# Second parts of the unsummed weights from ACT's negated copy and an adding transfer, and another set of paired FFN tiles, in a two-layer hybrid decoder step

## The chip, the core and the metric

The kernel runs on one core of one Trainium2 chip. The metric is the device time of one execution in microseconds (us). The time before is 1921.07 us, the median of three runs (1919.98 to 1923.55).

The core's engines work side by side, each through its own queue in order, and wait for each other on semaphores: TensorE (PE in the profile, its weight loads PEld), VectorE (DVE), ScalarE (ACT), GpSimd (POOL) and SyncE (SP). Transfers between the device memory and the core's memory are issued from the queues of SP, POOL or ACT and run on DMA engines that all queues share.

## The reference

One step of two layers over 520 tokens (512 prompt, 8 sample) of 1024 features. Cut to what matters:

```python
def swiglu_ffn(x, wg, wu, wd):
    return (jax.nn.silu(x @ wg) * (x @ wu)) @ wd

def layer(x, ...):
    x = x + 0.5 * swiglu_ffn(rms_norm(x, p['ffn1_norm']), p['ffn1_wg'], p['ffn1_wu'], p['ffn1_wd'])
    z = rms_norm(x, p['mix_norm']) @ p['w_in']
    # retention, windowed attention and a convolution on pieces of z, joined, times w_out
    x = x + y
    return x + 0.5 * swiglu_ffn(rms_norm(x, p['ffn2_norm']), p['ffn2_wg'], p['ffn2_wu'], p['ffn2_wd'])
```

So there are four FFNs (two in each layer), with a hidden width of 2816, and a mixing stage in each layer. All is in float32.

## The kernel before

**Two parts.** Each float32 operand of a matmul is split into a first part, rounded to float32r, and a second part, which is the rest: source minus first part. A product is three matmuls: first by second, first by first, second by first. ACT makes the first part of a weight (`split_hi`, line 290), DVE the second (`split_lo`, line 296).

**Weights** arrive from device memory in chunks of 128 x 1024 by SP's queue (line 245), into four buffers, in the order in which they are used (`seq` lists the units). A buffer is loaded again when its last unit has been split (`done`). The parts lie in six slots of 128 x 1024 (tags `wh` and `wl`, three buffers each). A plain chunk takes two slots, one for each part. A unit of a paired product takes one: 512 columns of the first part, then 512 of the second. `ahead(u)` runs at the start of a unit: it queues the first parts of units up to six slots on, and the second parts of those that were pending before. So the splitting of a unit's weights can begin when the product six slots earlier has been done.

**An FFN** has 22 hidden tiles of 128 features and three down projections, over tiles 0 to 7, 8 to 15 and 16 to 21, that stand behind hidden tiles 8, 16 and 21. A plain hidden tile (`hidden`) is 16 weight blocks times six matmuls of 260 columns, 96 in all. A paired tile (`pair_hidden`, the tiles in `PAIRED`, and the first two down projections through `pair_down`, four times each) goes by a scheme with seven products in place of eight (`seven`): a11, s1, s2, a12, s3, s4, a22, each of 12 matmuls, 84 in all. Three of them (a11, a12, a22) use a block of the weights as it is; s1, s2 and s4 use sums of blocks that DVE makes (`sums`, lines 258 to 263), s2's subtraction in place in the raw chunk, which s3 then uses. The inputs need sums as well (`input_sums`, `pair_blocks`, `sums4`), which DVE makes, ACT splits and DVE splits again, in steps that `advance` puts between the products.

**Order around a paired tile.** `seven` copies the sums between products by ACT (lines 518, 525, 530); the next product but one adds to the copy, so TensorE waits for it. `late` (lines 554 to 557) runs on DVE after the sixth product: for each of the two results t and u an addition from PSUM and a multiplication by R. `last` (line 561) reads the other halves after the seventh. Then `gated` runs SiLU on ACT (line 428) and a multiplication on DVE (line 430). PSUM has four tiles, of which a paired tile uses three. In a plain tile DVE reads the two results at lines 443 and 444.

**POOL** issues the loads of constants (line 193, after the first FFN of a layer has done its paired tiles) and some loads and stores of the mixing stage. It has nothing in the other parts of the FFNs.

Of the kernel before, what the change touches and what calls it, by code (L numbers as in the profile page):

```python
# [10 lines left out]
F32 = mybir.dt.float32  # L11
F32R = mybir.dt.float32r
AF = mybir.ActivationFunctionType
ALU = mybir.AluOpType
# [6 lines left out]
FFN = 2816  # L21
NF = FFN // 128

PAIRED = (4, 5, 6, 8, 9, 10, 12, 13, 14, 16, 17, 18, 20, 21)


GROUPS = ((0, 8, True), (8, 16, True), (16, 22, False))
# [5 lines left out]
PC = JP * 128  # L33
# [76 lines left out]
def ffn_steps():  # L110


    steps = [("hidden", f) for f in range(NF)]
    for n, g in reversed(list(enumerate(GROUPS))):
        steps.insert(min(g[1] + 1, NF), ("down", n))
    return steps
# [20 lines left out]
def step_kernel(ctx: ExitStack, tc: tile.TileContext, io: dict):  # L137
    nc = tc.nc
# [56 lines left out]
    def wt(name, n=NT, dt=F32, bufs=None):  # L195
        return work.tile([128, n], dt, tag="t", name=name)
# [7 lines left out]
    seq, slot = [], [0]  # L204
# [7 lines left out]
    def add_products(n):  # L212
        for _ in range(n):
            for name in PRODUCTS:
                seq.append((name, chunk[0]))
                slot.append(slot[-1] + 1)
            chunk[0] += 2

    chunk = [0]
    for _ in range(DEPTH):  # L220
        for part in range(3):
# [3 lines left out]
            for step, n in ffn_steps():  # L225
                if step == "hidden" and n in PAIRED:
                    add_products(1)
# [7 lines left out]
    raw, done, spl, ready = {}, set(), {}, set()  # L235
    at, nxt, loaded, pending = [0, 0], [0], [0], []

    def load(dma=True):

        while loaded[0] < NCH and (loaded[0] < RAW or loaded[0] - RAW in done):  # L240
            i = loaded[0]
            loaded[0] += 1
            raw[i] = wraw.tile([128, CT * 128], F32, tag="w", name="w")
            if dma:
                nc.sync.dma_start(raw[i], io["w"][i])

    def sums(u):

        if u >= len(seq) or u in ready:
            return  # L250
        ready.add(u)
        name, i = seq[u]
        if name == "chunk":
            return
        load()
        (a21, a11), (a22, a12) = ((raw[j][:, :PC], raw[j][:, PC:]) for j in (i, i + 1))
        if name == "s1":
            nc.vector.tensor_add(Rd[:, 0, :PC], a21, a22)
        elif name == "s2":
            nc.vector.tensor_sub(a21, a21, a11)  # L260
            nc.vector.tensor_add(Rd[:, 1, :PC], a21, a22)  # L261
        elif name == "s4":
            nc.vector.tensor_sub(Rd[:, 0, :PC], a12, Rd[:, 1, :PC])  # L263

    def source(u):
        name, i = seq[u]
        if name == "chunk":
            return raw[i]
        if name[0] == "a":
            return dict(a11=raw[i][:, PC:], a12=raw[i + 1][:, PC:], a22=raw[i + 1][:, :PC])[name]  # L270
        return raw[i][:, :PC] if name == "s3" else Rd[:, int(name == "s2"), :PC]

    def parts_of(u):

        tag = ("wh", "wl")
        if seq[u][0] == "chunk":
            return tuple(wspl.tile([128, CT * 128], F32R, tag=t, name=t) for t in tag)
        t = tag[slot[u] % 2]
        w = wspl.tile([128, CT * 128], F32R, tag=t, name=t)
        return w[:, :PC], w[:, PC:]  # L280

    def split_hi():

        u = nxt[0]
        if u < len(seq):
            nxt[0] += 1
            load()
            sums(u)
            spl[u] = parts_of(u)
            nc.scalar.copy(spl[u][0], source(u))  # L290
            pending.append(u)

    def split_lo(n=9):
        for u in pending[:n]:
            h, lo = spl[u]
            nc.vector.tensor_sub(lo, source(u), h.bitcast(F32))  # L296
            name, i = seq[u]
            if name in ("chunk", "s3", "a22"):
                done.add(i + (name == "a22"))
                load()  # L300
        del pending[:n]

    def ahead(u):

        old = len(pending)
        while nxt[0] < len(seq) and slot[nxt[0] + 1] - slot[u] <= 6:
            split_hi()
        if seq[u][0] == "chunk":
            split_lo()
        else:  # L310
            split_lo(old)
            sums(nxt[0])
            sums(nxt[0] + 1)
# [108 lines left out]
    def flush():  # L422
        while advance():
            pass
# [8 lines left out]
    def hidden(norm, first):  # L433

        og, ou = ptile(), ptile()
        for i, (o, k) in enumerate(ffn_tiles(first, og, ou)):
            mm3(o, next_tile(), xh[:, k], xl[:, k], k == 0, k == KD - 1)
            if i % 2:
                advance()
        if first:  # L440
            run(norm)
        t, u = wt("t"), wt("u")
        nc.vector.tensor_mul(v2(t), og[:, :, :HN], v2(R))  # L443
        nc.vector.tensor_mul(v2(u), ou[:, :, :HN], v2(R))  # L444
        return t, u
# [67 lines left out]
    def seven(blocks, late, last, early=None):  # L513

        one, mid, c22 = ptile(), ptile(), ptile()[:, 0, :HN]
        c11, c21, m5, c12 = (t[:, i, :HN] for t in (one, mid) for i in range(2))
        product("a11", c11, blocks, True)
        nc.scalar.copy(c22, c11)  # L518
        advance()
        product("s1", m5, blocks, True)  # L520
        if early:
            early(m5)
        advance()
        product("s2", c22, blocks, False)
        nc.scalar.copy(c12, c22)
        advance()
        product("a12", c11, blocks, False)
        advance()
        product("s3", c22, blocks, False)
        nc.scalar.copy(c21, c22)  # L530
        advance()
        product("s4", c12, blocks, False)
        late(c12, c22, m5)
        advance()
        product("a22", c21, blocks, False)
        advance()
        last(one)
# [13 lines left out]
    def pair_hidden(blocks):  # L551
        t, u, v = wt("t"), wt("u"), wt("v")[:, :HN]

        def late(c12, c22, m5):
            for d, c in ((t, c12), (u, c22)):
                nc.vector.tensor_add(d[:, HN:], c, v)
                nc.vector.tensor_mul(d[:, HN:], d[:, HN:], R[:, HN:])

        def last(one):
            for i, d in enumerate((t, u)):  # L560
                nc.vector.tensor_mul(d[:, :HN], one[:, i, :HN], R[:, :HN])  # L561

        seven(blocks, late, last, lambda m5: nc.scalar.copy(v, m5))
        return t, u

    def ffn(l, name, norm, after):
        hs, even, spare, xs = {n: [] for n in range(len(GROUPS))}, None, [], []
        for step, n in ffn_steps():
            if step == "hidden":
                g = next(i for i, (a, b, _) in enumerate(GROUPS) if a <= n < b)  # L570
                t, u = pair_hidden(xs) if n in PAIRED else hidden(norm, n == 0)
                flush()
# [29 lines left out]
    def mix(l, after):  # L602
# [586 lines left out]
        def chunk_hi():  # L1189
            while True:  # L1190
                split_hi()
                yield

        def chunk_lo():
            while True:
                split_lo(1)
                yield
# [70 lines left out]
    for step in START:  # L1268
        if step[0] == "h":
            half(half_split, int(step[1]))  # L1270
        elif step[0] == "c":
            split_hi()
            split_lo()
        elif step[0] == "x":
            next(parts[int(step[1])])
            next(parts[int(step[1])])
        else:
            run(parts[int(step[1])])
# [17 lines left out]
def host_arrays(i):  # L1296
# [17 lines left out]
    for t, j in zip(gu, (1, 2)):  # L1314
# [3 lines left out]
        for step, n in ffn_steps():  # L1318
            if step == "hidden":
                g = t[:, n]  # L1320
                if n in PAIRED:

# [96 lines left out]
```

## Time and profile before

| | |
|---|---|
| median of three runs | 1921.07 us |
| the profiled execution | 1921.25 us |
| its span, first to last instruction | 1919.5 us |
| mean granted TensorE clock | 0.986 |
| read from device memory, written | 179.50 MB, 7.45 MB |

The span is what the trace covers; 1.75 us of the profiled execution lie around it. A row of a group gives line, engine, operation, result and operands, shapes and count, then the busy time in us and the mean of one in ns, then the idle time of the engine just before these instructions and what ended most of it. A row of the waits gives the engine and line that waited, what it waited for, the total in us, how often, and the longest. A row of the timeline gives start and duration in us, and in brackets the idle time before. A row of the chain gives start and length in us, engine, line and count. Matmuls overlap in the records: the duration of one is longer than the distance to the next.

### The profile page before, as it was taken

The numbers are of one execution on the slowest core, as the hardware profiler recorded it, in microseconds if no ns is written. First come the engines' busy times: TensorE is split into PE (matmuls) and PEld (weight loads), VectorE is DVE, ScalarE is ACT, GpSimd is POOL, SyncE is SP. The second block draws the span as 40 slices with busy tenths as digits, with TensorE's granted clock in tenths as the row PEclk, the third lists the DMA queues.
The fourth block names the chain that finished last, engine by engine and source line by source line (L and its number), as shares of the span: only waits on it lengthen the run. The fifth ranks groups of instructions, "written<-read, shape, count | busy, mean of one in ns | idle before, by whom it ended". The sixth has DMA issues, their size and how long they took to land.

```text
span 1919.5 us, 37036 instructions
## 1 busy us (share of the span) xinstructions
PE 1844.9 (96%) x15134; PEld 1820.6 (95%) x15134; DVE 1584.9 (83%) x2743; ACT 999.2 (52%) x1880; POOL 23.3 (1%) x52
## 2 busy tenths in 40 slices
PE   8999999999989999999999999999998999999999
PEld 8999999999989999999999999999998999999998
DVE  8988998688667998998779989976886579888984
ACT  6544545433765555555455555555238555455552
POOL 0000000000100000000000000000000000000000
PEclk9999999999999999999999999999999999999999
DMA  5233333433313133333323232334333132232332
GB/s 180 78 90 99 100 99 111 138 108 114 116 38 96 56 101 109 97 91 100 110 78 89 89 110 89 120 112 127 100 116 100 45 99 73 83 111 89 102 97 89
DMA packets 54171, 189.36 MB, mean 99 GB/s; under 512 B 6272, under 2 KB 7152, under 8 KB 54000
## 3 DMA queue, kind: packets, MB, share of 16 engines
q1 hardware_dynamic: 50784, 177.35, 30.4%
q0 software_dynamic: 3072, 9.53, 1.5%
q8 instruction: 119, 1.95, 0.4%
q14 instruction: 52, 0.43, 0.1%
q10 hardware_dynamic: 144, 0.11, 0.0%
HBM read 179.50 MB, written 7.45 MB: 97 GB/s over the span
## 4 chain that ended last, share of the span: by engine, by line
PE 76%; DVE 16%; ACT 5%; issue 2%; DMA 1%; ACTq 0%; POOL 0%; DVEq 0%; POOLq 0%
PE o L342 40%; PE o L334 34%; DVE wl L296 2%; DVE m L474 2%; DVE wh L296 2%; DVE Rd L263 1%; DVE u L430 1%; DVE w L260 1%; ACT wh L290 1%; DVE m L502 1%; ACT wl L290 1%; ACT t L428 1%; PE o L361 1%; DVE u L444 1%; DVE Rd L261 0%
## 5 line engine op out<-in xcount | busy, mean ns | idle before, releaser
L334 PE MATMUL o<-m,wl 128*128 128x260 f32 x2688 | 370.4, 288 | 24.0 <-DVE t L443 10.6
L334 PE MATMUL o<-m,wh 128*128 128x260 f32 x2688 | 366.3, 286 | 24.1 <-ACT o L518 19.0
L334 PEld LDWEIGHTS o<-m,wl 128*128 128x128 f32 x2688 | 346.0, 193 | 29.7 <-issue 11.4
L342 PE MATMUL o<-xl,wh 128*128 128x260 f32 x1792 | 364.4, 285 | 6.7 <-DVE xl L387 5.9
L290 ACT CAST wh<-w 128x512 fp32r<-128x512 f32 (+1 forms) x318 | 257.1, 810 | 217.0 <-PE o L342 154.8
L334 PEld LDWEIGHTS o<-m,wh 128*128 128x128 f32 x2688 | 343.2, 191 | 27.4 <-ACT o L518 20.9
L342 PE MATMUL o<-xh,wl 128*128 128x260 f32 x1792 | 362.0, 284 | 0.1
L342 PE MATMUL o<-xh,wh 128*128 128x260 f32 x1792 | 361.8, 283 | 0.0
L342 PEld LDWEIGHTS o<-xl,wh 128*128 128x128 f32 x1792 | 277.9, 189 | 8.1 <-ACT wh L355 5.9
L342 PEld LDWEIGHTS o<-xh,wl 128*128 128x128 f32 x1792 | 277.5, 189 | 0.4 <-DVE wl L296 0.4
L342 PEld LDWEIGHTS o<-xh,wh 128*128 128x128 f32 x1792 | 277.0, 189 | 0.0
L296 DVE TENSOR_TENSOR wl<-w,wh 128x1024 fp32r<-128x1024 f32 x142 | 173.3, 1221 | 34.2 <-ACT wh L290 31.9
L342 PE MATMUL o<-m,wh 128*128 128x260 f32 x1024 | 164.5, 282 | 4.1 <-DVE m L510 4.1
L342 PEld LDWEIGHTS o<-m,wh 128*128 128x128 f32 x1024 | 140.0, 188 | 4.9 <-DVE m L510 4.9
L290 ACT CAST wl<-w 128x512 fp32r<-128x512 f32 x176 | 108.7, 618 | 54.3 <-PE o L342 34.0
L428 ACT ACTIVATE t<-t 128x520 f32<-128x520 f32 x88 | 56.1, 637 | 137.1 <-DVE t L561 136.9
L334 PE MATMUL o<-xh,wl 128*128 128x260 f32 x672 | 124.6, 283 | 0.0
L334 PE MATMUL o<-xh,wh 128*128 128x260 f32 x672 | 124.3, 282 | 0.0
L296 DVE TENSOR_TENSOR wh<-w,wh 128x512 fp32r<-128x512 f32 x176 | 120.1, 682 | 0.0
L296 DVE TENSOR_TENSOR wl<-w,wl 128x512 fp32r<-128x512 f32 x176 | 120.1, 682 | 0.0
L290 ACT CAST wh<-Rd 128x512 fp32r<-128x512 f32 x132 | 82.0, 621 | 68.4 <-PE o L334 29.8
L290 ACT CAST wl<-Rd 128x512 fp32r<-128x512 f32 x132 | 81.8, 620 | 64.6 <-PE o L334 37.7
(216 smaller groups left out, 2716.5 us busy)
## 6 DMA issues: line engine op xcount, KB each, us to landing
w<-in_w SPq DMA_DIRECT2D x318, 512.0 KB, 3.6
out_y<-x SPq DMA_DIRECT2D x8, 260.0 KB, 2.0
m<-in_cm POOLq DMA_DIRECT2D x4, 512.0 KB, 4.3
m<-in_s_ret SPq DMA_DIRECT2D x4, 512.0 KB, 5.1
m<-sc POOLq DMA_DIRECT2D x8, 256.0 KB, 4.4
out_o_rets<-m POOLq DMA_DIRECT2D x4, 512.0 KB, 3.5
x<-in_x SPq DMA_DIRECT2D x3, 520.0 KB, 6.9
w<-in_w SPq DMA_DIRECT2D x4, 256.0 KB, 5.2
```

Source lines behind the costliest of these rows:

```text
L260: nc.vector.tensor_sub(a21, a21, a11)
L263: nc.vector.tensor_sub(Rd[:, 0, :PC], a12, Rd[:, 1, :PC])
L290: nc.scalar.copy(spl[u][0], source(u))
L296: nc.vector.tensor_sub(lo, source(u), h.bitcast(F32))
L334: nc.tensor.matmul(o, lhsT=a[:, s], rhs=b, start=first and j == 0 and i == 0, stop=j == JP - 1 and i == 2, skip_group_check=True,)
L342: nc.tensor.matmul(o[:, s, :HN], lhsT=a, rhs=b[:, s * HN : (s + 1) * HN], start=first and i == 0, stop=last and i == 2,)
L361: nc.tensor.matmul(o[:, s, :HN], lhsT=w, rhs=v[:, s * HN : (s + 1) * HN], start=i == 0, stop=i == len(parts) - 1,)
L428: nc.scalar.activation(t, t, AF.Silu)
L430: nc.vector.tensor_mul(u, u, t)
L444: nc.vector.tensor_mul(v2(u), ou[:, :, :HN], v2(R))
L474: nc.vector.tensor_sub(tl[:, c], src, th[:, c].bitcast(F32))
L502: nc.vector.tensor_sub(lo, a, h.bitcast(F32))
```

## The change

For a11, a12 and a22, `split_hi` now has ACT write a second copy, of the source times -1, into the place of the second part. Rounded to float32r it is the negated first part. Then a transfer issued from POOL adds the same block of the weights from device memory onto it (`accum_op`), which leaves the weights minus the first part. `split_lo` no longer subtracts on DVE for these units. The sources of s1, s2, s3, s4 and of plain chunks are split as before.

`PAIRED` has 15 tiles in place of 14, and others: 5, 6, 7, 9 to 15 and 17 to 21. Plain are now 0 to 4, 8 and 16 (before: 0 to 3, 7, 11, 15 and 19). The host lays the weights out for it.

In `late`, both additions run before the two multiplications.

```diff
-PAIRED = (4, 5, 6, 8, 9, 10, 12, 13, 14, 16, 17, 18, 20, 21)
+PAIRED = (5, 6, 7, 9, 10, 11, 12, 13, 14, 15, 17, 18, 19, 20, 21)
...
             nc.scalar.copy(spl[u][0], source(u))
+            name, i = seq[u]
+            if name[0] == "a":
+                nc.scalar.activation(spl[u][1], source(u), AF.Copy, scale=-1.0)
+                i, c = i + (name != "a11"), 0 if name == "a22" else PC
+                nc.gpsimd.dma_start(spl[u][1], io["w"][i][:, c : c + PC], accum_op=ALU.add)
             pending.append(u)
...
             h, lo = spl[u]
-            nc.vector.tensor_sub(lo, source(u), h.bitcast(F32))
             name, i = seq[u]
+            if name[0] != "a":
+                nc.vector.tensor_sub(lo, source(u), h.bitcast(F32))
...
             for d, c in ((t, c12), (u, c22)):
                 nc.vector.tensor_add(d[:, HN:], c, v)
+            for d in (t, u):
                 nc.vector.tensor_mul(d[:, HN:], d[:, HN:], R[:, HN:])
```

## The prediction

> **What bounds the kernel now.** I read the page's busy times first, then its groups, then TensorE's own waits, then windows stage by stage, and last the timeline at one stall. From the page:
>
> ```profile
> PE 1844.9 (96%) x15134; PEld 1820.6 (95%) x15134; DVE 1584.9 (83%) x2743; ACT 999.2 (52%) x1880; POOL 23.3 (1%) x52
> ...
> L334 PE MATMUL o<-m,wl 128*128 128x260 f32 x2688 | 370.4, 288 | 24.0 <-DVE t L443 10.6
> L334 PE MATMUL o<-m,wh 128*128 128x260 f32 x2688 | 366.3, 286 | 24.1 <-ACT o L518 19.0
> ...
> L290 ACT CAST wl<-w 128x512 fp32r<-128x512 f32 x176 | 108.7, 618 | 54.3 <-PE o L342 34.0
> L428 ACT ACTIVATE t<-t 128x520 f32<-128x520 f32 x88 | 56.1, 637 | 137.1 <-DVE t L561 136.9
> ...
> L296 DVE TENSOR_TENSOR wh<-w,wh 128x512 fp32r<-128x512 f32 x176 | 120.1, 682 | 0.0
> L296 DVE TENSOR_TENSOR wl<-w,wl 128x512 fp32r<-128x512 f32 x176 | 120.1, 682 | 0.0
> ```
>
> TensorE is busy 96% of the span, so nothing can win more than its idle time, its half-clock stretches, and matmuls left out. The idle time that this change can touch stands before the paired products of L334: 24.0 + 24.1 = 48.1 us. TensorE's waits name who ends it:
>
> ```profile
> PE o L334 <- ACT o L518: 19.0, 8, 2.4
> PE o L334 <- DVE u L556: 13.2, 15, 1.0
> PE o L334 <- DVE t L443: 10.6, 4, 2.9
> ...
> PE o L334 <- ACT o L530: 3.2, 8, 0.4
> PE o L334 <- ACT o L525: 2.1, 7, 0.3
> ```
>
> Those are 42 stops. ACT is named most, though it is busy 52%; the timeline where the first down projection begins shows what holds it (DVE rows, then ACT, then PE):
>
> ```profile
> 112.73 0.69 DVE L296 TENSOR_TENSOR wl<-Rd,wl 128x512 fp32r<-128x512 f32 x1
> 113.34 0.69 DVE L296 TENSOR_TENSOR wh<-Rd,wh 128x512 fp32r<-128x512 f32 x1
> ...
> 115.00 0.43 DVE L557 TENSOR_TENSOR t<-t,R 128x260 f32<-128x260 f32 x1
> 115.34 0.42 DVE L556 TENSOR_TENSOR u<-o,v 128x260 f32<-128x260 f32 x1
> ...
> 116.14 1.30 DVE L474 TENSOR_TENSOR m<-u,m 128x520 fp32r<-128x520 f32 x2
> 117.37 0.69 DVE L296 TENSOR_TENSOR wl<-w,wl 128x512 fp32r<-128x512 f32 x1
> 117.97 0.42 DVE L561 TENSOR_TENSOR t<-o,R 128x260 f32<-128x260 f32 x1
> ```
>
> ```profile
> 118.42 0.64 ACT L428 ACTIVATE t<-t 128x520 f32<-128x520 f32 x1 [3.84 <-DVE t L561]
> ...
> 119.47 0.37 ACT L518 COPY o<-o 128x260 f32<-128x260 f32 x1
> ```
>
> ```profile
> 115.82 1.71 PE L334 MATMUL o<-m,wl 128*128 128x260 f32 x12 [1.02 <-DVE u L556]
> 119.89 0.80 PE L334 MATMUL o<-m,wh 128*128 128x260 f32 x2 [2.36 <-ACT o L518]
> ```
>
> DVE runs without a break and late: a weight subtraction (117.37) stands ahead of L561, SiLU on ACT waits 3.84 us for L561, the copy L518 is queued behind SiLU, and TensorE waits 2.36 us for the copy. So the bound behind these stops is DVE's backlog in paired stretches. The windows say so by stage (columns: length, busy us of PE, PEld, DVE, ACT, POOL, then granted clock, DMA share, GB/s):
>
> ```profile
> 158.88:244.84 85.96, 84.24 (x698) 83.62 (x697) 77.36 (x144) 46.05 (x95) 0.00 (x0) 1.00 0.34 99
> 113.20:158.90 45.70, 42.32 (x339) 41.90 (x338) 40.87 (x72) 22.45 (x44) 0.00 (x0) 0.96 0.31 93
> 830.70:874.90 44.20, 40.81 (x339) 40.39 (x338) 40.70 (x72) 22.45 (x44) 0.00 (x0) 1.00 0.33 96
> 54.80:70.60 15.80, 12.90 (x87) 12.72 (x86) 14.71 (x27) 10.29 (x22) 0.00 (x0) 0.78 0.21 67
> ```
>
> DVE is busy 77.36 of 85.96 us over FFN tiles 9 to 16 (six paired), 14.71 of 15.80 over the first paired tile. A stop also costs granted clock: two equal down projections took 45.70 us at clock 0.96 and 44.20 at 1.00.
>
> **The change, part by part.**
>
> ```profile
> 179.19 11.53 PE o L342 x96
> 837.41 57.75 PE o L334 x480
> ```
>
> *One more paired tile in each of four FFNs.* A plain tile is 96 matmuls, 11.53 us; a paired one 84, at 57.75/480 = 0.120 us each 10.1 us. 4 x 1.45 = **5.8 us less** TensorE work.
>
> *DVE's subtraction goes for a11, a12, a22.* Each set of seven products loses three of 682 ns; queued ones start 0.60 us apart (112.73, 113.34), so 1.8 us a set. For tiles 9 to 16, then seven paired: TensorE needs 7 x 10.1 + 11.5 = 82 us; DVE 77.4 - 6 x 1.8 + about 3.6 (a plain tile made paired: four small subtractions, five sums and six short evictions for two long subtractions and two evictions) = 70 us, 86% where it had 90%, and the down projection falls from 40.9 by 4 x 1.8 to 33.7 us of 40.3. Backlogs drain within a tile instead of over four. The first paired tile is now the sixth: its 10.6 us of waits on L443 meet a DVE that had one more plain tile to catch up.
>
> *What the stops are worth.* 48.1 us are counted from the modelled end of the matmul before; a matmul lasts 0.286 and the next could start after 0.120, so each of the 42 stops hides 0.166 more: 7 us. Half clock: 1.5 us (45.70 against 44.20) in about five of eight down projections, and 0.22 of 15.80 us in the first paired tile, partly under idle time, four times: estimate 12 us together. At stake: 48 + 7 + 12 = 67 us. I let 10 stay (alternate tiles still carry four or more microseconds of input sums on DVE).
>
> A rule of the Trainium skill speaks against the 12: "TensorE: Matmul & The Clock Gate", section "HAM oscillation", says that only idle gaps over about 3.4 us bring the clock down. The longest stop above is 2.9 us and the clock is down at 0.96 and 0.78 around such stops, so the trace disagrees; by the Trainium skill's rule the 12 us would stay, and the sum be 1876.
>
> *`late` reordered.* The second L556 starts one L557 sooner: 0.34 us (115.00 to 115.34) at up to 15 stops, part of the 13.2 us above, not counted again.
>
> *ACT's negated copy.* 92 sets x 3 = 276 more instructions. None has this form in the trace; nearest are the cast of equal size, 618 ns, and an ACTIVATE, 637. I take 0.62; queued casts start 0.52 apart (108.92, 109.44 below). That is 1.6 us a set. Tiles 9 to 16: 46.0 + 21 x 0.52 + about 3 for the new paired tile = 60 of 82 us, so there is room. But ACT is in order: the copies L518, L525, L530 and SiLU come up to 0.5 us later. TensorE has one product (12 x 0.12 = 1.44 us) between a copy's input and its use, which covers it; without cover, 0.5 us x 92 sets = 46 us. I take 3.
>
> *The accumulating transfer.* It waits for the negated copy and TensorE's third matmul of the product waits for it. POOL has nothing else in the FFNs but the two constant loads after the first FFN's paired tiles; what queues behind a waiting issue is the next accumulate. SP's loads share the 16 DMA engines: share 0.34 at 99 GB/s, to which 3 x 262 KB per 10.1 us (78 GB/s) add 0.27 if plain, 0.54 if reading the destination counts double. So there is room, with queueing. What matters is the time from ACT to use:
>
> ```profile
> 106.09 0.60 ACT L290 CAST wl<-w 128x512 fp32r<-128x512 f32 x1
> ...
> 106.87 0.62 ACT L290 CAST wh<-w 128x512 fp32r<-128x512 f32 x1
> ...
> 108.92 0.62 ACT L290 CAST wl<-Rd 128x512 fp32r<-128x512 f32 x1
> 109.44 0.62 ACT L290 CAST wh<-Rd 128x512 fp32r<-128x512 f32 x1
> ```
>
> ```profile
> 111.77 1.61 PE L334 MATMUL o<-m,wl 128*128 128x260 f32 x12
> 113.21 0.28 PE L334 MATMUL o<-m,wh 128*128 128x260 f32 x1
> ```
>
> The cast of a22 ends at 106.69; a22's product starts at 111.77, its third matmul 0.24 later: 5.3 us. Less 0.52 for the negated copy: 4.8, and some 0.1 for waking: **4.7 us** from POOL's issue to the landing. The next a11 (106.87 to 113.45) has 5.96, less two copies, 4.9. In a down projection SiLU and the copy of v aren't ahead: about 1 us more, 5.8.
>
> ```profile
> m<-sc POOLq DMA_DIRECT2D x8, 256.0 KB, 4.4
> out_o_rets<-m POOLq DMA_DIRECT2D x4, 512.0 KB, 3.5
> ```
>
> ```profile
> DMA to landing us min/median/max: 3.4/4.4/5.8
> ```
>
> ```profile
> DMA to landing us min/median/max: 2.9/3.5/4.2
> ```
>
> No accumulate is in the trace. These are the page's rows of POOL's transfers, then the same two lines' own views (L1015, L1027): 256 KB in bursts of four land in 3.4 to 5.8 us, 512 KB alone in 2.9 to 4.2. An accumulate of 256 KB reads 512 KB: I take 4.0 us, nearest the lone 512 KB, and add 3 us over the kernel for late ones. Ends: 2.9 costs nothing, and none can gain, since only a late one is seen; 5.8 costs (5.8 - 4.7) x 60 hidden sets = 66 us, all of the gain; beyond the rows it can be more.
>
> The Trainium skill, "DMA: Bandwidth & Descriptors", section "Anatomy of one DMA", gives 2.0 us plus bytes over 436 GB/s: an estimate of 2.6 us for 256 KB, 3.2 for 512. The lone 512 KB rows lie at and above it; by it no transfer would be late and the sum would be 3 us lower. No run here shows an accumulate.
>
> **The sum.** The profiled execution took 1921.25 us: 1919.5 span and 1.75 around it, 0.2 over the median of 1921.07. 1921.3 - 5.8 - 67 + 10 + 3 + 3 = **1864.5 us**.
>
> **The rivals.**
> (a) *Slower: the accumulates land late.* Slot u's second part can't be begun until the product six back is done, so lateness isn't absorbed by a deeper queue: TensorE stops once a set. For it: 4.7 us is close to the 4.4 median, two issues 0.8 us apart overlap, SP's 512 KB share the engines, and an adding transfer may run below a copy's rate. Against: lone transfers land well inside. It decides from a landing of 4.7 + 57/60 = 5.65 us. At 7.0 (twice 3.5): 2.3 x 60 + 1.2 x 32 = 176 us, 1864.5 + 176 = 2040.
> (b) *Somewhat late*, landing at 5.2: 0.5 x 60 = 30, 1895.
> (c) *ACT takes the place of DVE.* The 24.3 us of stops that ACT ends (19.0 + 3.2 + 2.1) stay, with some 10 of the 7 + 12 us that go with stops: 1864.5 + 35 = 1900. For it: ten weight casts a set in one ordered queue with SiLU. Against: 60 of 82 us, and its 3.84 us wait was for DVE.
> (d) *Given back*: landing near 5.6, or long waits that move: 1921.
> (e) *The clock doesn't recover*: the half-clock stretches have another cause than these stops and stay, 1864.5 + 12 = 1876. That one of two equal stages was spared (44.20 against 45.70 us) with the same stops speaks for it, that they begin around stops against it. The rule of the Trainium skill above is this rival's.
> (f) *The backlog wasn't it*: stops come from a fixed chain of latencies. DVE's unbroken rows from 112.73 on speak against it; only 5.8 + 5 go: 1910. Counted with (c).
>
> **Chances.** Forecast 0.45 (1844 to 1885: 1848.5 with every stop gone and nothing late, 5 below for gaps too short for the rows; 20 above for twice the stops left and 10 us of lateness); (a) 0.21; (b) 0.14; (c) and (f) 0.09; (d) 0.07; (e) 0.04. Two kernels closer than 0.2% (3.8 us) can't be told apart. Faster 0.45 + 0.14 + 0.09 + 0.04 = 0.72, same 0.07, slower 0.21. The range 1844 to 1937 takes in all but most of (a).
>
> **What would show it.** Right: no L296 row for w of 512 columns but s3's 92; L334's idle time near 10 us and no L518 wait over 1 us; DVE near 1440 us busy, ACT near 1150; 276 new POOL issues landing near 4 us; clock 1.00 in the down projections. Wrong: TensorE's waits released by those transfers; many stops of equal length, one a set, at a22's or a11's third matmul (a); L518 still ahead in its waits while SiLU no longer waits for DVE (c). I would be wrong above all if an adding transfer takes over 5.6 us.

## The result, and the profile after

| | time, us | ratio to before |
|---|---|---|
| before, median of 4 | 1920.76 | 1 |
| changed, median of 4 | 1983.84 (1978.28 to 1986.45) | 1.0322, 95% interval 1.0308 to 1.0336 |

The changed kernel is 3.2% slower; 1864.5 us was forecast, and the time lies outside the range. The page of the changed kernel (its line 342 is the old 334, 350 the old 342, 305 the old 296; 295 is the negated copy, 297 the adding transfer):

```profile
span 1984.6 us, 37952 instructions
...
PE 1853.9 (93%) x15086; PEld 1815.2 (91%) x15086; DVE 1450.6 (73%) x2519; ACT 1156.3 (58%) x2192; POOL 262.0 (13%) x328
...
q1 hardware_dynamic: 50784, 177.35, 30.7%
q0 software_dynamic: 42816, 81.90, 24.6%
...
w<-in_w SPq DMA_DIRECT2D x318, 512.0 KB, 3.7
wh<-in_w POOLq DMA_DIRECT2D x138, 256.0 KB, 5.9
wl<-in_w POOLq DMA_DIRECT2D x138, 256.0 KB, 6.0
```

DVE and ACT are as busy as the prediction said (about 1440 and 1150 us). But TensorE, which has 48 matmuls fewer, idles 131 us of the span where it idled 75, and the adding transfers land in 5.9 to 6.0 us, not 4.0. TensorE's waits in the changed kernel:

```profile
PE o L342 <- DMA wl<-in_w: 55.5, 47, 2.3
PE o L342 <- DMA wh<-in_w: 48.8, 45, 2.0
...
PE o L342 <- ACT o L526: 3.5, 12, 0.4
```

The old waits for DVE's `t` and `u` before paired products are gone, and of those for ACT's copies 3.5 us are left. In their place stand 92 waits for the transfers, 104.3 us. Taken transfer by transfer, 85 of them (101.5 us) are at a22's product, each in another of the 92 sets of seven products; five are at a11's and two at a12's. With the 0.166 us that each stop hides (as worked out in the prediction) that is 104.3 + 92 x 0.166 = 119.6 us. The time measured is 1983.8 - 1864.5 = 119.3 us over the forecast. So the loss by the transfers is of the size of the whole miss; that the two agree this closely is partly luck, as e2 below shows.

One set in the timeline of the changed kernel, hidden tile 10: first ACT, then POOL, then SP, then TensorE.

```profile
175.78 0.61 ACT L290 CAST wh<-w 128x512 fp32r<-128x512 f32 x1
176.29 0.63 ACT L295 ACTIVATE wh<-w 128x512 fp32r<-128x512 f32 x1
```

```profile
177.22 0.86 POOL L297 DMA_DIRECT2D wh<-in_w  x1 [5.72 <-ACT v L572]
178.54 0.86 POOL L297 DMA_DIRECT2D wl<-in_w  x1 [0.45 <-ACT o L533]
183.92 0.86 POOL L297 DMA_DIRECT2D wh<-in_w  x1 [4.52 <-ACT wh L295]
```

```profile
174.93 2.35 SPq L245 DMA_DIRECT2D w<-in_w  x2
```

```profile
183.32 0.39 PE L342 MATMUL o<-m,wh 128*128 128x260 f32 x1 [0.95 <-DMA wh<-in_w]
```

a22's copy is done at 176.92, POOL issues at 177.22, 0.30 us later where 0.1 was allowed. TensorE stops until 183.3, at the third matmul of a22. SP's two weight loads of 512 KB go out between 174.93 and 177.28. The landing of the three transfers above, in order, each from the view of its own line and moment:

```profile
DMA to landing us min/median/max: 6.1/6.1/6.1
DMA to landing us min/median/max: 6.1/6.1/6.1
DMA to landing us min/median/max: 4.0/4.0/4.0
```

a22's and the next a11's take 6.1, a12's 4.0. The first two lie beside SP's loads, the third alone. It is so throughout: in all 92 sets two loads were in flight when a22's transfer was issued, the later one sent 0.27 us (median) before it. By the trace's issues and landings the medians are 6.3 us for a22's transfers, 6.4 for a11's and 4.25 for a12's.

### The profile page after: what moved, and what is told of

Its sections match the earlier page's. It is cut to its first block, busy times and chain, and to the rows that moved or that the text cites. A ratio compares the mean times of both kernels' runs of the same rounds, so it can differ in the third digit from the quotient of the medians.

```text
span 1984.6 us, 37952 instructions
## 1 busy us (share of the span) xinstructions
PE 1853.9 (93%) x15086; PEld 1815.2 (91%) x15086; DVE 1450.6 (73%) x2519; ACT 1156.3 (58%) x2192; POOL 262.0 (13%) x328
## 3 DMA queue, kind: packets, MB, share of 16 engines
q1 hardware_dynamic: 50784, 177.35, 30.7%
q0 software_dynamic: 42816, 81.90, 24.6%
## 5 line engine op out<-in xcount | busy, mean ns | idle before, releaser
L342 PE MATMUL o<-m,wl 128*128 128x260 f32 x2784 | 388.5, 286 | 56.2 <-DMA wl<-in_w 54.4
L342 PE MATMUL o<-m,wh 128*128 128x260 f32 x2784 | 388.1, 286 | 50.0 <-DMA wh<-in_w 47.8
L350 PE MATMUL o<-xl,wh 128*128 128x260 f32 x1664 | 337.9, 284 | 6.8 <-DVE xl L395 5.8
L350 PEld LDWEIGHTS o<-xl,wh 128*128 128x128 f32 x1664 | 257.4, 189 | 8.0 <-ACT wh L363 5.8
L350 PEld LDWEIGHTS o<-xh,wl 128*128 128x128 f32 x1664 | 257.0, 189 | 0.3 <-DVE wl L305 0.3
L350 PEld LDWEIGHTS o<-xh,wh 128*128 128x128 f32 x1664 | 256.8, 189 | 0.0
L297 POOL DMA_DIRECT2D wl<-in_w x138 | 119.7, 867 | 708.9 <-ACT wl L295 486.5
L297 POOL DMA_DIRECT2D wh<-in_w x138 | 119.7, 868 | 624.4 <-ACT wh L295 308.2
L350 PE MATMUL o<-m,wh 128*128 128x260 f32 x1024 | 164.1, 282 | 0.0
L550 DVE SCALAR_TENSOR_TENSOR x<-o,x 128x520 f32<-128x520 f32 (+1 forms) x128 | 72.0, 563 | 71.8 <-PE o L342 70.7
L305 DVE TENSOR_TENSOR wh<-Rd,wh 128x512 fp32r<-128x512 f32 x138 | 94.9, 688 | 37.2 <-ACT wh L290 35.6
```

The source lines that it names most:

```text
L297: nc.gpsimd.dma_start(spl[u][1], io["w"][i][:, c : c + PC], accum_op=ALU.add)
L342: nc.tensor.matmul(o, lhsT=a[:, s], rhs=b, start=first and j == 0 and i == 0, stop=j == JP - 1 and i == 2, skip_group_check=True,)
L350: nc.tensor.matmul(o[:, s, :HN], lhsT=a, rhs=b[:, s * HN : (s + 1) * HN], start=first and i == 0, stop=last and i == 2,)
L550: nc.vector.scalar_tensor_tensor(d, src, 0.5, d, op0=ALU.mult, op1=ALU.add)
```

## The experiments

All from the changed kernel, unless said. The theory at first was that the loss is lateness, from sharing the DMA engines; the rivals were the set of tiles, the adding itself, and POOL's issue path.

**e1, no adding transfers.** The new set and the new order in `late`, with all second parts by DVE.

```diff
-            if name[0] == "a":
+            if name in ():
...
-            if name[0] != "a":
+            if name not in ():
```

> The new set of paired tiles and the new order in late, all second parts by DVE again, no adding transfers. Theory T (the loss is lateness of the adding transfers, which share the DMA engines with SP's weight loads; the set itself is harmless): no stop by a transfer; DVE needs some 11.5 us a paired tile against 10.1 on TensorE, so seven in a row run late, but the first paired tile's 16 us are gone: 1905 to 1930 us. Rival S (the set with seven paired tiles in a row is what costs): 1950 us or more.

1896.9 us, ratio 0.9869 (0.9855 to 0.9884): faster than before by 1.3%, and 8 us better than the best end expected. The set is no cost. The granted clock is 0.995 here, where it was 0.986 before. DVE's backlog still stops TensorE, less than before:

```profile
PE o L342 <- DVE u L564: 12.5, 16, 1.3
PE o L342 <- DVE t L451: 10.0, 8, 1.5
PE o L342 <- ACT o L526: 10.0, 9, 1.2
```

So rival S falls. From before to e1, TensorE's busy time falls by 15.4 us, of which the forecast gave 5.8 to the matmuls left out, and its idle time from 74.6 to 65.0 us. From the page of e1:

```profile
PE 1829.5 (97%) x15086; PEld 1802.5 (95%) x15086; DVE 1594.2 (84%) x2795; ACT 1017.4 (54%) x1916; POOL 23.3 (1%) x52
```

**e2, a11 and a12 by transfers, a22 by DVE.**

```diff
-            if name[0] == "a":
+            if name in ("a11", "a12"):
...
-            if name[0] != "a":
+            if name not in ("a11", "a12"):
```

> As the changed kernel, but a22's second part by DVE again; 184 adding transfers instead of 276. T: the stop at a22's third matmul (about 1.1 us, 92 times) is gone, a11's transfer no longer has a neighbour 1.3 us away and lands in about 5 us instead of 6.4: 1870 to 1905 us. Rival A (an adding transfer is slow by itself, whatever lies beside it): a11 lands at 6.4 us and takes over a22's stops: 1950 us or more.

1868.33 us (1867.23 to 1869.45), ratio 0.9718 (0.9702 to 0.9734): better than both kernels, and 1.7 us under the range expected. The page's landings are

```profile
wh<-in_w POOLq DMA_DIRECT2D x92, 256.0 KB, 4.2
wl<-in_w POOLq DMA_DIRECT2D x92, 256.0 KB, 4.4
```

and TensorE's waits at the paired products are

```profile
PE o L342 <- DMA wh<-in_w: 5.6, 11, 1.3
PE o L342 <- DMA wl<-in_w: 5.3, 8, 1.1
PE o L342 <- ACT o L526: 4.7, 12, 1.1
```

that is 10.9 us for transfers, in 19 stops. The page's landings mix two kinds: a12's transfers landed in 4.1 us (median), a11's, still beside the loads in most sets, in 5.1, where they had taken 6.4. That is mostly in time: at the 17 stops which a11's transfers caused, their lead was about 5.5 us (median). Rival A, that an adding transfer is slow wherever it stands, falls as the main cause.

**e3, copying in place of adding.**

```diff
-                nc.gpsimd.dma_start(spl[u][1], io["w"][i][:, c : c + PC], accum_op=ALU.add)
+                nc.gpsimd.dma_start(spl[u][1], io["w"][i][:, c : c + PC])
```

> As the changed kernel, but the 276 transfers copy instead of adding, so the second parts of a11, a12 and a22 hold the weights themselves. T and A: the transfers read half as much; packets take about 84 ns instead of 178, those beside loads land in about 4.5 us: 1860 to 1885 us. Rival P (POOL's issue path, 0.87 us an issue and a fixed delay, is what is slow): landing stays at 6 us, 1975 to 1990 us.

1903.06 us (1897.83 to 1913.31): 18 us over the range of T and A, a miss, but far below P's, and the landings are not P's 6 us either: P falls as the main cause. The page of e3:

```profile
q0 software_dynamic: 42816, 81.90, 15.0%
...
wh<-in_w POOLq DMA_DIRECT2D x138, 256.0 KB, 4.5
wl<-in_w POOLq DMA_DIRECT2D x138, 256.0 KB, 4.4
```

Before, POOL's queue took 1.5% of 1919.5 us, 29 us of all 16 engines. An adding transfer therefore takes (24.6% x 1984.6 - 29)/276 = 1.66 us of them, a copying one (15.0% x 1896.1 - 29)/276 = 0.92; a 512 KB load, by q1's 30.7% for 177.35 MB, 1.8 us. So to the engines an adding 256 KB is nearly a 512 KB load. Copies too landed late at times: 30 stops, 26 us, 28 of them at a22's products, where the copies took 5.2 us (median) and a12's, clear of the loads, 2.9.

**e4, the loads held back.** Both loads of a set wait for a memset of one column on DVE, behind the sixth product; the calls of `load` in `split_lo`, `split_hi` and `sums` are left to plain chunks, or to a chunk that is missing.

```diff
+            if mark:
+                nc.vector.memset(raw[i][:, :1], 0.0)
             if dma:
                 nc.sync.dma_start(raw[i], io["w"][i])
...
         late(c12, c22, m5)
+        load(mark=True)
```

> As the changed kernel, but the two weight loads of a paired product set are held back by a one-column memset on DVE until after the sixth product, some 4 to 5 us later, so that they do not run beside the transfers of a22 and the next a11. T: these land in 4.2 to 4.8 us instead of 6.4, a12's transfer meets a load instead and lands in 5 to 6, within its 5.8: 1870 to 1910 us. A and P: no change, 1975 to 1990 us.

2119.66 us (2108.61 to 2131.41), ratio 1.1027: expected 1870 to 1910, a miss. The median landing did fall, to 4.2 us on the page (a22's alone: 4.8). But the weights themselves came too late; DVE's first wait in e4 is

```profile
DVE Rd L261 <- DMA w<-in_w: 337.1, 76, 6.9
```

With four chunk buffers, two sets, there is no room to hold a load for that long. The run speaks for the landing, not for the time.

**e5, a12 and a22 by transfers, a11 by DVE** (edit as in e2, with the other names).

> As the changed kernel, but a11's second part by DVE again; a22 and a12 by adding transfers, each without a neighbour 1.3 us away. Theory N (three transfers are too many because the two neighbours and SP's loads share the DMA engines): a22 lands in 4.2 us alone to 5.2 beside loads, against a lead of about 4.5, so stops of 0 to 0.7 us in 60 hidden sets: 1870 to 1905 us. Rival B (a22's place is what costs, since its lead is the shortest): its stops of 1.1 us stay in all 92 sets, 1950 us or more.

1949.77 us (1947.17 to 1954.13): nearly as rival B said, 92 stops, 83.8 us, 91 of them at a22's products:

```profile
PE o L342 <- DMA wl<-in_w: 43.0, 47, 2.4
PE o L342 <- DMA wh<-in_w: 40.8, 45, 2.7
```

Three transfers are thus not too many by their number: two are slower than the kernel before as well, if a22's is one of them. Theory N as it was put falls. By the trace's issues and landings, a22's 92 transfers, all issued with two loads in flight, took 6.1 us (median), and a12's 92, issued with one or none, 4.06. For a22 no neighbour of POOL's is needed; the loads do most of it (with a11's behind it, in the changed kernel, it took 6.3).

**e6, the old set with all three transfers** (only `PAIRED` undone).

> All three adding transfers and the new order in late, with the old set of 14 paired tiles. N: the stops at a22 are of the transfers' own making, one in each of 88 sets, 1.1 to 1.3 us: 1970 to 2000 us. Rival S (seven paired tiles in a row make the transfers late): 1930 us or less, since paired tiles stand three in a row at most.

1994.58 us, ratio 1.0388 (1.0366 to 1.0409): as expected; 85 stops, 97.7 us. The set has no part in the lateness.

**e7, the kernel before with the new order in `late` alone.**

> The kernel before with the new order in late alone. By the prediction's working the second addition starts 0.34 us earlier at up to 15 stops: 5 us less, 1914 to 1918 us. Rival: the stop moves to the next item of DVE's backlog, 1919 to 1922 us.

1915.19 us, ratio 0.9967 (0.9955 to 0.9979), as expected. The waits for `u` fell from 13.2 us:

```profile
PE o L334 <- DVE u L556: 7.3, 13, 0.8
```

**e8, e2 with a transfer that nothing waits for** at a22's place: 512 KB copied within device memory, by the same sum as in e3 about 1.8 us of all 16 engines. ACT's copy of a22 is made and DVE overwrites it; the one-column copy on POOL makes the transfer wait for it, as a22's did.

```diff
+            if name == "a22":
+                nc.scalar.activation(spl[u][1], source(u), AF.Copy, scale=-1.0)
+                nc.gpsimd.tensor_copy(tiny, spl[u][1][:, :1].bitcast(F32))
+                z = junk.tile([128, 1024], F32, tag="z", name="z")
+                nc.gpsimd.dma_start(z, io["w"][i + 1])
```

> As e2 (a11 and a12 by adding transfers, a22 by DVE), and at the place of a22's transfer POOL issues one that nothing waits for: 512 KB of the weights copied within device memory, which takes about the DMA engines' time of an adding 256 KB; ACT's negated copy of a22 is made too, and not used. N: a11's transfer lands in 5.5 to 6.5 us instead of 4.2 and TensorE stops for it, 1900 to 1960 us. B: 1868 to 1880 us, since nothing waits for the transfer at a22's place.

1993.27 us (1988.45 to 1996.87): 125 us over e2 for something that nobody needs, even more than expected. a11's transfer lands in 6.2 us (median; 5.1 in e2). TensorE now stops for the transfers that e2 had in time:

```profile
PE o L349 <- DMA wl<-in_w: 51.7, 39, 3.5
PE o L349 <- DMA wh<-in_w: 40.8, 36, 2.5
```

72 of these 75 stops are at a11's products. So lateness comes from other traffic on the DMA engines. B as it was put, that a22's lead alone is what is short, falls too. What was left: a transfer is late when it lies beside the loads, the more so with another transfer of POOL's there.

**e9, the loads held back less,** until behind the fourth product (`load(mark=True)` there, the rest as in e4).

> All three adding transfers as in the changed kernel; the two weight loads of a paired set are held back by a one-column memset on DVE until the fourth product, some 2 to 3 us later than they went, and 3 us earlier than in e4. Theory L (SP's load waits for the same last reader as a22's transfer, ACT's copy of a22, so both start together; kept apart, the transfers are in time): a22 and a11 land in 4.1 to 4.8 us and the stop at a22 goes; a12 meets the loads and lands in 5.5 to 6.2 against a lead of 5.5: 1870 to 1930 us. Rival B (a22's lead is too short for any adding transfer): stops at a22 stay, 1970 us or more.

2063.51 us (2057.81 to 2073.64), another miss in time: both loads now go out together, at once with the next a11's transfer. From the timeline of e9, POOL's rows and SP's:

```profile
194.63 0.86 POOL L301 DMA_DIRECT2D wl<-in_w  x1 [4.45 <-ACT v L578]
195.95 0.86 POOL L301 DMA_DIRECT2D wh<-in_w  x1 [0.45 <-ACT o L538]
```

```profile
196.26 0.87 SPq L247 DMA_DIRECT2D w<-in_w  x2
```

The landings of these two, a22's and the next a11's, from their line's view:

```profile
DMA to landing us min/median/max: 4.4/4.4/4.4
DMA to landing us min/median/max: 7.2/7.2/7.2
```

a22, 1.6 us ahead of the loads, lands in 4.4 us, and a11, beside them, in 7.2. TensorE waits 153.3 us for transfers, in this stretch at a11's products and no longer at a22's. Over the whole run a22's transfer was issued with no load in flight in 66 sets, 4 of which stopped for it, and with one or two in 26, 21 of which did; a11's products have 65 stops. The late one moved with the loads: L holds in its mechanism, B falls, and the time expected was wrong because the hold moved the collision instead of ending it.

**e10, a12 alone by a transfer.**

> One adding transfer a set, a12's; a11 and a22 by DVE. L: a12 has the longest lead and stands clear of the loads, so TensorE stops for it hardly at all; DVE is relieved of 0.6 us a set in place of 1.2: between e1 and e2, nearer e2, 1868 to 1885 us. Rival D (it is DVE's whole relief that counts): halfway or worse, 1885 to 1897 us.

1875.66 us (1873.58 to 1878.77), ratio 0.9759 (0.9745 to 0.9774), as L expected. TensorE stops for them 16 times, 8.5 us. They land alike:

```profile
DMA to landing us min/median/max: 3.9/4.1/4.8
```

## Why the prediction was wrong

**The step that failed** is the landing of the adding transfer: "I take 4.0 us, nearest the lone 512 KB, and add 3 us over the kernel for late ones". Alone it lands in 4.1 us (e10; a12's in the changed kernel in 4.25), so the size was right for a lone one; a22's, at which nearly all stops are, took 6.3. The step before it, "So there is room, with queueing", weighed the DMA engines by their mean share. The share was indeed moderate, over the seven paired tiles 9 to 15 0.71, where the prediction had 0.61 to 0.88:

```profile
161.52:246.58 85.06, 75.39 (x590) 73.92 (x589) 63.64 (x125) 56.37 (x116) 17.28 (x20) 0.96 0.71 154
```

What counts is what lies beside the transfer in its own 5 us, and the prediction did not ask what sets the loads off: SP's two loads of a set wait for the last readers of their buffers, and the last reader of the second one is the split of a22. Before, that was DVE's subtraction, and SP's own waits name it:

```profile
SPq L245 <- DVE wl L296: 1170.2, 216, 33.6
SPq L245 <- DVE wh L296: 516.2, 88, 20.8
```

The change itself makes it ACT's negated copy, the same event that lets a22's transfer go. In the changed kernel SP's waits name these copies, and the copy right behind them on ACT, beside DVE (56 + 18 + 18 = 92, one for each set):

```profile
SPq L245 <- ACT v L572: 94.7, 56, 3.0
...
SPq L245 <- ACT wh L295: 23.9, 18, 2.3
SPq L245 <- ACT wl L295: 22.3, 18, 2.3
```

Two loads of 1.8 us each and two adding transfers of 1.66, 6.9 us of work for all 16 engines, meet within some 4 us. e8 (a copy of about the same work for the engines, with no one waiting for it, makes a11's late) and e9 (loads moved, so another transfer late) show this; e2 shows that without a22's part in it the rest is mostly in time. The "3 us over the kernel for late ones" were 119.6.

**Rival (a)** is what happened, with its point of decision, 5.65 us: the landings of 5.9 to 6.0 lie over it. Its price was put too low for that landing: (6.0 - 4.7) x 60 + (6.0 - 5.8) x 32 = 84 us, where the stops cost 119.6. The lead, from POOL's issue to where the third matmul could have begun, was not the reason in the hidden sets: at the stops it was 5.0 us (median), though POOL took 0.30 us to wake and not 0.1. But a22's own landing is above the page's, as a12's pulls that down (6.2 on average in the hidden sets, 6.5 in the down projections), and in the down projections the lead was 5.5 and not 5.8, so that 29 of their 32 sets stop for a22's as well. One reading in the prediction is not right: of the lone 512 KB rows the least, 2.9 us, lies below the estimate of 3.2, not at or above it.

**Right, and confirmed by a run of its own:** DVE's backlog was the bound behind the stops. From e1 to e2 the stops that DVE and ACT end before paired products shrink from 39.7 us to 4.7, ACT's with DVE's. e2 takes 1868.3 us, 3.8 from the 1864.5 of the sum, but it has only two of the three transfers and still 10.9 + 19 x 0.166 = 14 us of stops by them: without these it would take some 1854, so the sum was somewhat too high, and the closeness here is luck. So is, in part, that of 119.6 to 119.3 above: the stops also lowered the changed kernel's clock, to 0.989, which the 119.6 leaves out. The first down projection took 41.04 us in e2, where it took 45.70:

```profile
109.56:150.60 41.04, 40.73 (x338) 40.49 (x337) 33.07 (x54) 25.69 (x50) 6.91 (x8) 1.00 0.64 149
```

The half-clock share of the sum held there too: 1.00 in this window against 0.96, and 0.995 over e2's span against 0.986. But it came with the new set, not with DVE's relief: e1 has 0.995 already, with stops of 39.7 us before paired products but none over 1.53 us, where the longest before was 2.9; e7 has 0.985. So rival (e) falls. The traces thus again speak against the rule of the Trainium skill as the prediction read it ("TensorE: Matmul & The Clock Gate", section "HAM oscillation"): no stop before paired products was over 3.4 us, and yet the clock rose when those of over 2 us went. `late` gave 6 us, where 0.34 us at 15 stops had been said. ACT's copy took 0.63 us (0.62 taken), and ACT did not become the bound, so (c) falls: its copies end 3.5 us of waits. (f) falls by e2.

**Mis-sized:** what the new set does without the transfers. The set and `late` gave 1922.5 - 1896.9 = 25.6 us (e1), `late` about 6 of them; so the set gives nearly 20 with DVE unrelieved, and DVE's relief by two transfers a further 28.6. The prediction gave nearly all of this to DVE's relief; a part of it is the set's own. By e1's page most of these 20 us are TensorE's busy time, 15.4 us less: about 6 by fewer matmuls and the rest, by the clock, by shorter ones. The set's plain tiles now stand ahead of the first paired tile and of two down projections, where DVE can catch up before the paired products begin; which of these places counts was not tried.

**Left open:** a version with all three transfers in time was not found. Eight slots in place of six, which would let a weight's split begin earlier, were not tried.

## What to carry to other kernels

Moving work to a transfer buys engine time and pays in latency: compare the lead in the timeline with the landing beside whatever the other queues send in the same few microseconds, not with a lone landing or a mean share. Look at what event sets off each transfer; a load that refills the buffer which the same split has just freed will run beside it, here in all 92 sets. And try a part of the change: with two of the three transfers the kernel gained 2.8% where with all three it lost 3.2%, with one alone 2.4%; 1.3% of each gain is the new set and `late`.

## What was unexpected of the hardware

An adding transfer costs POOL more to issue, 0.86 us where copies of the same size take 0.53 (from the views of line 297, min, median and max in ns, of the changed kernel and then of e3):

```profile
L297 POOL DMA_DIRECT2D wh<-in_w x138: 854/863/1177, 56.3 to 1932.7; - x138
```

```profile
L297 POOL DMA_DIRECT2D wh<-in_w x138: 527/527/667, 56.4 to 1845.6; - x138
```

It also lands later than a copy, by about as much alone as beside the loads: 4.25 us against 2.9 for a12's (medians, the changed kernel and e3), 6.3 against 5.2 for a22's. Single ones took 9.7 us (e9).
